# Feed-forward stage 1 with one 512-column matmul for the high weight part, and PSUM as four tiles of two banks

## The chip, the cores and the metric

The kernel runs on one core of one Trainium2 chip. The time is device microseconds of one execution. Before the change the median of three runs is 1102.05 us (1101.83 to 1103.43).

## The reference

Two layers of a decoder trunk, batch 1, 256 tokens (S), model width 1024 (D), all in float32. Layer 0 is a feed-forward block, native sparse attention (NSA) and a feed-forward block; layer 1 is a feed-forward block, differential attention and a feed-forward block:

```
x = x + 1/2 FFN1(rmsnorm(x)); x = x + Mixer(rmsnorm(x)); x = x + 1/2 FFN2(rmsnorm(x))

def swiglu(x, w_in, w_out):
    a, b = jnp.split(x @ w_in, 2, axis=-1)
    return (jax.nn.silu(a) * b) @ w_out
```

`w_in` is 1024 x 5632 (a gate half and an up half, 2816 each), `w_out` is 2816 x 1024. The change is in `x @ w_in`, which occurs four times, and in how PSUM is declared for the whole program.

## The kernel before

**Precision.** Every float32 product is made of three matmuls. A value is split in a high part (rounded to float32r) and a low part (value minus high part), and `mm3` issues high x high, low x high and high x low into the same accumulator (L359, L360, L361; `mm3x` is the same for stage 2 at L364 to L366).

**Weights.** `Stream` loads chunks of 128 x 2048 words by the SP queue into three buffers. ACT casts the high part (`whi`, L86, four pieces of 128x512), DVE and POOL make the low part (`wlo`, L89 and L91); how many columns of a piece go to POOL is set by `W.pool`, which is 0 in the inner pairs of a feed-forward block.

**Activations.** x is held transposed, as eight k-tiles of 128 rows by 256 tokens. `Norm` holds g * x as `xhi` and `xlo`, two tiles. 1/rms is applied after stage 1, by multiplying with `rb`, which has the same row in every partition. `Norm.bank` makes the parts of two k-tiles (ACT `xhi` L327, DVE `xlo` L328), the squares (ACT L334) and their sum (POOL L336, L338).

**Feed-forward (`ffn`).** The 2816 hidden units are 11 pairs p of 256. `stage1(p)` is 8 k-tiles x 2 halves j of the pair x gate and up (c) x three matmuls of 256 columns: 96 matmuls into two PSUM banks, each with gate and up side by side. The banks alternate: 4 and 5 for even p, 6 and 7 for odd p. `evac(p)` multiplies a bank by `rb` on DVE (`ab`, L401), takes Silu on ACT (`sh`, L403), multiplies by the up half on DVE (L405), and splits the result in `hh` (ACT, L407) and `hl` (DVE, L409). `stage2(p)` is 48 matmuls of 256 columns that add to banks 0 to 3 over all pairs (24 of 512 columns in the last block). The program issues stage1(p), evac(p), stage2(p-1) for each p, so on TensorE the stage 2 of one pair lies between two stages 1, and evac(p) has that time to come through. At the end of a block `residual_bank` adds each bank to x (DVE, L370) and calls `Norm.bank` for the next stage.

**Order and PSUM.** The framework orders the instructions of each engine by the priorities that come from program order, and places the semaphore waits from the tiles that the instructions read and write. PSUM is eight tiles of one bank, `B[0]` to `B[7]`. The mixers use the same tiles. In NSA `kc_t` transposes the compressed keys into `B[2 + tb]`, bank 2 and bank 3 in turn (L618), and DVE adds a position term out of that bank (`kc`, L622); the head loops transpose probabilities (L882) into one bank while DVE and ACT copy from others (L884, L885, L904).

Of the kernel before, what the change touches and what calls it, by code (L numbers as in the profile page):

```python
# [17 lines left out]
P = 128  # L18
# [38 lines left out]
class Stream:  # L57
    """Weight chunks of 128 x 2048 words, loaded and split ahead of their use."""

# [64 lines left out]
def trunk_kernel(ctx, tc, x, ffn1_norm, ffn1_w_in, ffn1_w_out, mix_norm, ffn2_norm, ffn2_w_in, ffn2_w_out,  # L124
# [10 lines left out]
    pp = pool("pp", 1, space=bass.MemoryType.PSUM)  # L135
    B = [pp.tile([P, 512], F32, name=f"bank{i}") for i in range(8)]

# [159 lines left out]
    def rsqrt(h, n, out=None, np_=P):  # L297
        """1 / sqrt(-2 h), for h < 0."""
        y, a = out if out is not None else tiny("ry", n)[:np_], (tiny if n <= 32 else t2)("ra", n)[:np_]
        nc.vector.tensor_scalar(y.bitcast(I32), h.bitcast(I32), -0.5, 0x5F1FFFF9 - 0x40400000, op0=ALU.mult, op1=ALU.add)  # L300
        beta = 3 * 0.703952253
        nc.vector.scalar_tensor_tensor(a, y, beta, y, op0=ALU.mult, op1=ALU.mult)
        nc.vector.tensor_tensor(a, a, h, op=ALU.mult)
        nc.vector.scalar_tensor_tensor(y, a, beta * 2.38924456 / 2, y, op0=ALU.add, op1=ALU.mult)
        nc.vector.scalar_tensor_tensor(a, y, 4.0 / 9.0, y, op0=ALU.mult, op1=ALU.mult)
        nc.vector.tensor_tensor(a, a, h, op=ALU.mult)
        nc.vector.scalar_tensor_tensor(a, a, 5.0 / 3.0, a, op0=ALU.add, op1=ALU.mult)
        nc.vector.scalar_tensor_tensor(y, a, 1.25, y, op0=ALU.add, op1=ALU.mult)
        return y

    class Norm:
        """Holds g * x^T as two float32r parts, and 1 / rms of each token."""

        def __init__(self, g0):
            self.g0 = g0
            self.hi = xp.tile([P, KT, S], F32R, tag="xhi", name=nm("xhi"))
            self.lo = xp.tile([P, KT, S], F32R, tag="xlo", name=nm("xlo"))
            self.acc = t2("acc")
# [21 lines left out]
        def rms(self, ps):  # L340
            """1 / rms as a column."""
            for tb in range(2):
# [7 lines left out]
        def rms_row(self, ps):  # L350
            """1 / rms along the free dimension, the same in every partition."""
            nc.tensor.matmul(ps[:, :S], ones, self.acc[:, :S], start=True, stop=True)
# [20 lines left out]
    def ffn(nrm, nxt_g, last=False, first=False):  # L373
        hbuf = {}
        xn = None

        def stage1(p):
            gs = [B[4 + 2 * (p % 2)], B[5 + 2 * (p % 2)]]
            for half in range(2):
# [3 lines left out]
                for kk in range(4):  # L383
                    k = half * 4 + kk
                    for j in range(2):
                        for c in range(2):
                            mm3(gs[j][:, c * S:(c + 1) * S], hv[:, kk, c, j * P:(j + 1) * P], lv[:, kk, c, j * P:(j + 1) * P],
                                nrm.hi[:, k, :], nrm.lo[:, k, :], k == 0 and c == 0, k == KT - 1)
                    if p == 0 and k == (7 if first else 6):
                        nrm.rms_row(B[0])  # L390
                    if p == 1 and k == (3 if first else 1):
                        evac(0)

        def evac(p):
            gs = [B[4 + 2 * (p % 2)], B[5 + 2 * (p % 2)]]
            hh = halves(t2("hh", 512, F32R), 2)
# [3 lines left out]
            for j in range(2):  # L400
                nc.vector.tensor_tensor(halves(ab[j], 2), halves(gs[j], 2), nrm.rb[:, None, :].to_broadcast([P, 2, S]), op=ALU.mult)  # L401
            for j in range(2):
# [9 lines left out]
        def stage2(p, nxt=None):  # L412
# [5 lines left out]
            if last:  # L418
                for tb, c0, c1 in ((0, 0, 512), (0, 512, 1024), (1, 0, 512)) + (((1, 512, 768), (1, 768, 1024)) if end else ((1, 512, 1024),)):
                        yb = B[2 * tb + c0 // 512][:, c0 % 512:c0 % 512 + c1 - c0]  # L420
# [9 lines left out]
                return  # L430
            for d in range(KT):
                for j in range(2):
                    mm3x(B[d // 2][:, (d % 2) * S:(d % 2 + 1) * S], hv[:, j, d * P:(d + 1) * P], lv[:, j, d * P:(d + 1) * P],
                        hh[:, j, :], hl[:, j, :], p == 0 and j == 0 and d % 2 == 0, end and j == 1)
                if end and d % 2:
                    residual_bank(d // 2, 0.5, nxt)

        for p in range(NPAIR):
            W.pool = FFN_SPLIT if p in (0, NPAIR - 1) or first and p == 1 else 0
            stage1(p)  # L440
            if p:
                evac(p)
            if p == NPAIR - 1 and first:
                setup_late2(B[4 + 2 * ((p + 1) % 2)])
            if p == 0 and last:
# [9 lines left out]
            if p:  # L455
                stage2(p - 1)
        if last:
            stage2(NPAIR - 1)
# [5 lines left out]
    def proj(key, nrm, segs, split):  # L464
        """Yields after each tile of the model dimension; segs[tb]: (psum, width, opens its bank)."""
        tot = sum(sg[1] for sg in segs[0])
# [34 lines left out]
    def qk_factors(b, nrm, r2, fac):  # L501
        """Per token and head of the raw projection: the norm's factor, and its inverse."""
        ss = tiny("ss", 16)
# [96 lines left out]
    def nsa(nrm, nxt_g):  # L600
# [209 lines left out]
        def filler():  # L810
            for k in proj("q1", nrm, full(0), (4, 4)):
                yield
            qhl1 = q_parts(0, xp.tile([P, 2048], F32R, tag="xlo", name=nm("qhl")), 1)
            yield
# [343 lines left out]
```

## Time and profile before

| | us |
|---|---|
| median of 3 runs | 1102.05 |
| span of the profiled execution | 1109.3 |
| TensorE (PE) busy | 1066.8 (96%) |
| DVE busy | 786.5 (71%) |
| ACT busy | 563.8 (51%) |
| POOL busy | 297.9 (27%) |
| mean granted TensorE clock | 0.973 of full speed |

The profiled execution has no time of its own beside its span: the span, from its first to its last instruction, is 1109.3 us, 7.25 us (0.7%) above the median of the runs. PE's busy time includes overlap of neighbouring matmuls, so the distance from one matmul's start to the next says more than a matmul's duration.

### The profile page before, as it was taken

The page shows a single profiled execution, that of the slowest core. Times are in us where ns is not written, and L with a number is a line of the kernel's source. Part 1 is how long each engine was busy: PE and PEld are TensorE (multiplying, and loading weights), DVE is VectorE, ACT ScalarE, POOL GpSimd, SP SyncE. Part 2 cuts the span into 40 slices and gives each one's busy share as a digit, 9 for nine tenths or more (in the row PEclk, how much of TensorE's full clock was granted, in tenths as well). Part 3 has the DMA queues.
Part 4 walks back from the last instruction along what each step waited for, and adds up shares of the span by engine and source line. Part 5 has one row for each costly group of instructions (what it writes and reads, how often), then busy time and mean ns, then how long its engine had stood idle before and what let it go on. Part 6 is the DMA issues. An engine that isn't in the chain of part 4 may idle for free.

```text
span 1109.3 us, 20061 instructions
## 1 busy us (share of the span) xinstructions
PE 1066.8 (96%) x7766; PEld 992.1 (89%) x7766; DVE 786.5 (71%) x1638; ACT 563.8 (51%) x1231; POOL 297.9 (27%) x350
## 2 busy tenths in 40 slices
PE   8899999998899999999999999999998989999998
PEld 7799999877767899999999999998776689999997
DVE  6865655889887796655689556568877789565664
ACT  6344444546587654444455444446454456444442
POOL 5500001766653240000073000017575434000002
PEclk9899999998899999999999999999998799999999
DMA  7655564477411256565565655654533225656551
GB/s 231 201 191 191 183 198 159 145 152 203 146 39 39 77 170 211 184 196 182 163 188 170 210 191 161 198 174 157 190 115 113 77 77 166 203 165 198 182 189 39
DMA packets 129980, 178.20 MB, mean 161 GB/s; under 512 B 5162, under 2 KB 104668, under 8 KB 129884
## 3 DMA queue, kind: packets, MB, share of 16 engines
q1 hardware_dynamic: 129708, 176.84, 50.4%
q8 instruction: 61, 1.00, 0.4%
q14 instruction: 35, 0.29, 0.1%
q10 hardware_dynamic: 176, 0.07, 0.0%
HBM read 175.84 MB, written 1.05 MB: 159 GB/s over the span
## 4 chain that ended last, share of the span: by engine, by line
PE 75%; DVE 17%; issue 3%; ACT 3%; POOL 1%; DMA 1%; SPq 0%; ACTq 0%; POOLq 0%; DVEq 0%
PE bank L360 18%; PE bank L359 18%; PE bank L361 18%; DVE wlo L89 6%; PE bank L366 5%; PE bank L364 5%; PE bank L365 5%; PE bank L901 1%; DVE xlo L328 1%; ACT whi L86 1%; PE bank L882 1%; PE bank L1038 1%; PE bank L849 1%; DMA xnat<-in_x_dram 1%; DVE kc L622 1%
## 5 line engine op out<-in xcount | busy, mean ns | idle before, releaser
L89 DVE TENSOR_TENSOR wlo<-raw,whi 128x512 fp32r<-128x512 f32 (+5 forms) x661 | 429.8, 688 | 189.0 <-ACT whi L86 187.7
L86 ACT CAST whi<-raw 128x512 fp32r<-128x512 f32 (+1 forms) x661 | 374.8, 618 | 362.8 <-issue 325.0
L91 POOL TENSOR_TENSOR wlo<-raw,whi 128x320 fp32r<-128x320 f32 (+4 forms) x240 | 229.9, 983 | 718.0 <-ACT whi L86 713.4
L361 PE MATMUL bank<-xhi,wlo 128*128 128x256 f32 x1408 | 397.7, 283 | 0.0
L360 PE MATMUL bank<-xlo,whi 128*128 128x256 f32 x1408 | 397.7, 282 | 0.0
L359 PE MATMUL bank<-xhi,whi 128*128 128x256 f32 x1408 | 397.7, 283 | 0.0
L359 PEld LDWEIGHTS bank<-xhi,whi 128*128 128x128 f32 x1408 | 266.1, 189 | 0.7 <-ACT xhi L327 0.2
L360 PEld LDWEIGHTS bank<-xlo,whi 128*128 128x128 f32 x1408 | 265.7, 189 | 0.7 <-DVE xlo L328 0.2
L361 PEld LDWEIGHTS bank<-xhi,wlo 128*128 128x128 f32 x1408 | 265.7, 189 | 0.0
L364 PE MATMUL bank<-hh,whi 128*128 128x256 f32 x528 | 150.5, 285 | 4.1 <-ACT hh L407 4.1
L366 PE MATMUL bank<-hl,whi 128*128 128x256 f32 x528 | 150.6, 285 | 1.3 <-DVE hl L409 1.3
L365 PE MATMUL bank<-hh,wlo 128*128 128x256 f32 x528 | 150.0, 284 | 0.0
L401 DVE TENSOR_TENSOR ab<-bank,rb 128x512 f32<-128x512 f32 x88 | 60.3, 691 | 67.6 <-PE bank L361 66.7
L364 PEld LDWEIGHTS bank<-hh,whi 128*128 128x128 f32 x528 | 102.0, 193 | 4.4 <-ACT hh L407 4.3
L366 PEld LDWEIGHTS bank<-hl,whi 128*128 128x128 f32 x528 | 101.9, 193 | 1.9 <-DVE hl L409 1.9
L365 PEld LDWEIGHTS bank<-hh,wlo 128*128 128x128 f32 x528 | 102.0, 193 | 0.0
L359 PE MATMUL bank<-whi,xhi 128*128 128x512 f32 (+1 forms) x192 | 78.9, 411 | 1.2 <-DVE kTl L645 1.2
L360 PE MATMUL bank<-wlo,xhi 128*128 128x512 f32 (+1 forms) x192 | 76.3, 398 | 3.0 <-DVE wlo L89 3.0
L361 PE MATMUL bank<-whi,xlo 128*128 128x512 f32 (+1 forms) x192 | 76.0, 396 | 0.0
L529 ACT ACTIVATE p<-p,mn 128x128 f32<-128x128 f32 (+1 forms) x96 | 43.0, 450 | 26.0 <-DVE mn L528 25.7
L403 ACT ACTIVATE sh<-ab 128x256 f32<-128x256 f32 x88 | 36.4, 413 | 23.0 <-DVE ab L401 23.0
L360 PEld LDWEIGHTS bank<-wlo,xhi 128*128 128x128 f32 x192 | 38.4, 200 | 10.3 <-issue 3.9
(242 smaller groups left out, 1274.7 us busy)
## 6 DMA issues: line engine op xcount, KB each, us to landing
raw<-in_ffn_w_in_dram SPq DMA_DIRECT2D x174, 512.0 KB, 4.8
raw<-in_ffn_w_out_dram SPq DMA_DIRECT2D x44, 1024.0 KB, 4.9
raw<-in_diff_w_in_dram SPq DMA_DIRECT2D x12, 1024.0 KB, 5.3
raw<-in_nsa_w_in_dram SPq DMA_DIRECT2D x6, 1024.0 KB, 5.2
raw<-in_nsa_cmp_w_dram SPq DMA_DIRECT2D x8, 512.0 KB, 7.1
raw<-in_nsa_w_out_dram SPq DMA_DIRECT2D x4, 1024.0 KB, 5.4
raw<-in_diff_w_out_dram SPq DMA_DIRECT2D x4, 1024.0 KB, 5.0
raw<-in_nsa_w_in_dram SPq DMA_DIRECT2D x4, 512.0 KB
```

The source lines that it names most:

```text
L86: self.nc.scalar.copy(hi[:, a:b], raw[:, a:b])
L89: self.nc.vector.tensor_tensor(lo[:, a:m], raw[:, a:m], hi[:, a:m].bitcast(F32), op=ALU.subtract)
L91: self.nc.gpsimd.tensor_tensor(lo[:, m:b], raw[:, m:b], hi[:, m:b].bitcast(F32), op=ALU.subtract)
L359: nc.tensor.matmul(ps, wh, xh, start=start, stop=False, skip_group_check=True)
L360: nc.tensor.matmul(ps, wh, xl, start=False, stop=False, skip_group_check=True)
L361: nc.tensor.matmul(ps, wl, xh, start=False, stop=stop, skip_group_check=True)
L364: nc.tensor.matmul(ps, wh, xh, start=start, stop=False, skip_group_check=True)
L365: nc.tensor.matmul(ps, wl, xh, start=False, stop=False, skip_group_check=True)
L366: nc.tensor.matmul(ps, wh, xl, start=False, stop=stop, skip_group_check=True)
L401: nc.vector.tensor_tensor(halves(ab[j], 2), halves(gs[j], 2), nrm.rb[:, None, :].to_broadcast([P, 2, S]), op=ALU.mult)
L403: nc.scalar.activation(sh[j][:, :S], ab[j][:, :S], AF.Silu)
L529: nc.scalar.activation(p, p, AF.Exp, bias=mn, scale=-1.0, accum_out=sm)
```

## The change

PSUM is declared as four tiles of two banks (`pair`), and `B[i]` is now a half of such a tile. The high and low parts of g * x become one tile `both`, in which the two parts of a k-tile lie side by side, 512 columns.

For p of 1 and up, stage 1 issues two matmuls instead of three for each k-tile, j and c: the high weight part times high and low activations together, 512 columns into a whole bank, and the low weight part times the high activations, 256 columns into the first half of that bank. A pair then takes four banks: one pair tile per j, gate in its first bank and up in its second. Those tiles are banks 4 to 7 for every p from 2 on (banks 0, 1, 6, 7 for p = 1), where before two sets alternated. In `evac` ACT first copies the low halves of a pair tile into `sh`, DVE adds them to the other halves, and the multiplication by `rb` then reads the sum from SBUF. Pair 0 keeps the three matmuls, into banks 4 and 5.

Around it: `rms_row` uses bank 2; stage2(0) begins with banks 2 and 3; the last stage 2 of a block runs all eight d for j = 0 first and then for j = 1 with the residuals; `setup_late2` (the transposes at L271 and L273) moves behind stage2(9); in `nsa` a buffer takes the new tag and size.

```diff
-    B = [pp.tile([P, 512], F32, name=f"bank{i}") for i in range(8)]
+    pair = [pp.tile([P, 1024], F32, name=f"bank{2 * i}") for i in range(4)]
+    B = [pair[i // 2][:, i % 2 * 512:(i % 2 + 1) * 512] for i in range(8)]
...
-            self.hi = xp.tile([P, KT, S], F32R, tag="xhi", name=nm("xhi"))
-            self.lo = xp.tile([P, KT, S], F32R, tag="xlo", name=nm("xlo"))
+            self.both = xp.tile([P, KT, 2, S], F32R, tag="xhl", name=nm("xhl"))
+            self.hi, self.lo = self.both[:, :, 0], self.both[:, :, 1]
...
+        def gate_up(p):
+
+            return [pair[0] if p == 1 else pair[2], pair[3]]
+
...
-                            mm3(gs[j][:, c * S:(c + 1) * S], hv[:, kk, c, j * P:(j + 1) * P], lv[:, kk, c, j * P:(j + 1) * P],
-                                nrm.hi[:, k, :], nrm.lo[:, k, :], k == 0 and c == 0, k == KT - 1)
+                            wh, wl = hv[:, kk, c, j * P:(j + 1) * P], lv[:, kk, c, j * P:(j + 1) * P]
+                            if p == 0:
+                                mm3(B[4 + j][:, c * S:(c + 1) * S], wh, wl,
+                                    nrm.hi[:, k, :], nrm.lo[:, k, :], k == 0 and c == 0, k == KT - 1)
+                                continue
+                            g = gate_up(p)[j][:, c * 512:(c + 1) * 512]
+                            nc.tensor.matmul(g, wh, nrm.both[:, k].rearrange("p c t -> p (c t)"),
+                                             start=k == 0, stop=False, skip_group_check=True)
+                            nc.tensor.matmul(g[:, :S], wl, nrm.hi[:, k, :], start=False, stop=k == KT - 1,
+                                             skip_group_check=True)
                     if p == 0 and k == (7 if first else 6):
-                        nrm.rms_row(B[0])
+                        nrm.rms_row(B[2])
...
-                nc.vector.tensor_tensor(halves(ab[j], 2), halves(gs[j], 2), nrm.rb[:, None, :].to_broadcast([P, 2, S]), op=ALU.mult)
+                src = halves(B[4 + j], 2)
+                if p:
+                    g = gate_up(p)[j].rearrange("p (c x t) -> p c x t", c=2, x=2)
+                    nc.scalar.copy(halves(sh[j], 2), g[:, :, 1])
+                    nc.vector.tensor_tensor(halves(ab[j], 2), g[:, :, 0], halves(sh[j], 2), op=ALU.add)
+                    src = halves(ab[j], 2)
+                nc.vector.tensor_tensor(halves(ab[j], 2), src, nrm.rb[:, None, :].to_broadcast([P, 2, S]), op=ALU.mult)
...
+            order = [*range(4, KT), *range(4)] if p == 0 else [*range(KT)]
+            for js in ((0,), (1,)) if end else ((0, 1),):
+                for d in order:
+                    for j in js:
+                        mm3x(B[d // 2][:, (d % 2) * S:(d % 2 + 1) * S], hv[:, j, d * P:(d + 1) * P], lv[:, j, d * P:(d + 1) * P],
+                             hh[:, j, :], hl[:, j, :], p == 0 and j == 0 and d % 2 == 0, end and j == 1)
+                    if end and j == 1 and d % 2:
+                        residual_bank(d // 2, 0.5, nxt)
```

**The evacuation of a pair on DVE.** Inside the first block, between two stages 1, DVE works on one pair's banks and on pieces of the next chunks (`wlo15` is one of those). Before:

```order
L401 TENSOR_TENSOR ab_40_1113<-bank4_86,rb_12_340 128x512
L401 TENSOR_TENSOR ab_41_1114<-bank5_87,rb_12_340 128x512
L89 TENSOR_TENSOR wlo15_1128<-raw15_939,whi15_1127 128x512
L405 TENSOR_TENSOR sh_42_1115<-sh_42_1115,ab_40_1113 128x256
L89 TENSOR_TENSOR wlo15_1128<-raw15_939,whi15_1127 128x512
L405 TENSOR_TENSOR sh_43_1116<-sh_43_1116,ab_41_1114 128x256
L409 TENSOR_TENSOR hl_39_1112<-sh_42_1115,hh_38_1111 128x256
L89 TENSOR_TENSOR wlo15_1128<-raw15_939,whi15_1127 128x512
L409 TENSOR_TENSOR hl_39_1112<-sh_43_1116,hh_38_1111 128x256
```

With the change, at the same pair (L416 is the added sum, L418 the multiplication by `rb`, L422 and L426 are the old L405 and L409):

```order
L416 TENSOR_TENSOR ab_39_992<-bank4_84,sh_41_994 128x512
L89 TENSOR_TENSOR wlo15_1011<-raw15_850,whi15_1010 128x512
L418 TENSOR_TENSOR ab_39_992<-ab_39_992,rb_11_335 128x512
L416 TENSOR_TENSOR ab_40_993<-bank6_85,sh_42_995 128x512
L422 TENSOR_TENSOR sh_41_994<-sh_41_994,ab_39_992 128x256
L418 TENSOR_TENSOR ab_40_993<-ab_40_993,rb_11_335 128x512
L426 TENSOR_TENSOR hl_38_991<-sh_41_994,hh_37_990 128x256
L89 TENSOR_TENSOR wlo15_1011<-raw15_850,whi15_1010 128x512
L422 TENSOR_TENSOR sh_42_995<-sh_42_995,ab_40_993 128x256
L89 TENSOR_TENSOR wlo15_1011<-raw15_850,whi15_1010 128x512
L426 TENSOR_TENSOR hl_38_991<-sh_42_995,hh_37_990 128x256
```

Two sums have come in, the last reads of the banks are now the two sums, and `hl` stands two operations further back.

**The end of a block on DVE.** After the last stage 2 of the first block DVE adds the banks to `xT` (L370) and makes the low parts (L328), with pieces of the next weights between. Before:

```order
L370 SCALAR_TENSOR_TENSOR xT_104<-bank0_82,xT_104 128x512
L89 TENSOR_TENSOR wlo34_2397<-raw34_2190,whi34_2396 128x192 x2
L328 SCALAR_TENSOR_TENSOR xlo_81_2394<-xT_104,gcol_94,xhi_80_2393 128x256
L370 SCALAR_TENSOR_TENSOR xT_104<-bank1_83,xT_104 128x512
L328 SCALAR_TENSOR_TENSOR xlo_81_2394<-xT_104,gcol_94,xhi_80_2393 128x256
L370 SCALAR_TENSOR_TENSOR xT_104<-bank2_84,xT_104 128x512
L328 SCALAR_TENSOR_TENSOR xlo_81_2394<-xT_104,gcol_94,xhi_80_2393 128x256 x4
L370 SCALAR_TENSOR_TENSOR xT_104<-bank3_85,xT_104 128x512
```

With the change (L371 and L329 are the old L370 and L328; `bank0` and `bank2` are tiles of two banks):

```order
L89 TENSOR_TENSOR wlo34_2111<-raw34_1933,whi34_2110 128x192 x3
L371 SCALAR_TENSOR_TENSOR xT_100<-bank0_82,xT_100 128x512
L371 SCALAR_TENSOR_TENSOR xT_100<-bank2_83,xT_100 128x512
L329 SCALAR_TENSOR_TENSOR xhl_79_2108<-xT_100,gcol_90,xhl_79_2108 128x256 x2
L371 SCALAR_TENSOR_TENSOR xT_100<-bank0_82,xT_100 128x512
L329 SCALAR_TENSOR_TENSOR xhl_79_2108<-xT_100,gcol_90,xhl_79_2108 128x256 x2
L371 SCALAR_TENSOR_TENSOR xT_100<-bank2_83,xT_100 128x512
```

The weight pieces now stand ahead of the first residual, and the second residual is that of the other pair tile: TensorE finishes bank 0, then bank 2, then banks 1 and 3.

**The transposes of the compressed keys on TensorE.** In the NSA prelude four sets of four transposes (L618) lie between the matmuls of the key projection (`whi36` is its second chunk). The first two sets before the change:

```order
L618 MATMUL bank2_84<-cst_91,kcn_90_2590 128x128 x4
L359 MATMUL bank6_88<-whi36_2532,xhi_80_2393 128x512
L360 MATMUL bank6_88<-wlo36_2533,xhi_80_2393 128x512
L361 MATMUL bank6_88<-whi36_2532,xlo_81_2394 128x512
L359 MATMUL bank7_89<-whi36_2532,xhi_80_2393 128x512
L360 MATMUL bank7_89<-wlo36_2533,xhi_80_2393 128x512
L361 MATMUL bank7_89<-whi36_2532,xlo_81_2394 128x512
L618 MATMUL bank3_85<-cst_91,kcn_90_2590 128x128 x4
```

With the change (L638 is the old L618), the second and the third set:

```order
L638 MATMUL bank2_83<-cst_87,kcn_88_2304 128x128 x4
L360 MATMUL bank6_85<-whi36_2246,xhl_79_2108 128x512
L361 MATMUL bank6_85<-wlo36_2247,xhl_79_2108 128x512
L362 MATMUL bank6_85<-whi36_2246,xhl_79_2108 128x512
L360 MATMUL bank6_85<-whi36_2246,xhl_79_2108 128x512
L361 MATMUL bank6_85<-wlo36_2247,xhl_79_2108 128x512
L362 MATMUL bank6_85<-whi36_2246,xhl_79_2108 128x512
L360 MATMUL bank6_85<-whi36_2246,xhl_79_2108 128x512
L638 MATMUL bank2_83<-cst_87,kcn_88_2304 128x128 x4
L361 MATMUL bank6_85<-wlo36_2247,xhl_79_2108 128x512
L362 MATMUL bank6_85<-whi36_2246,xhl_79_2108 128x512
```

Between the first and the second set nine matmuls stand now instead of six, and between the later ones seven. All four sets write the one tile `bank2`, in its first or its second bank, and in the built program each set from the second on carries a wait for DVE's reads of the set before it; before, the third and the fourth set waited for the reads of the set two before, in the same bank. The same kind of wait, for reads of the other bank of a pair tile, stands at 53 matmuls or transposes of TensorE, 21 instructions of ACT and 6 of DVE in the changed program; with eight tiles there was none.

## Rows read from the trace of the kernel before

**Rows 1.** The page: engines, and the chain that ended last.

```profile
PE 1066.8 (96%) x7766; PEld 992.1 (89%) x7766; DVE 786.5 (71%) x1638; ACT 563.8 (51%) x1231; POOL 297.9 (27%) x350
PE 75%; DVE 17%; issue 3%; ACT 3%; POOL 1%; DMA 1%; SPq 0%; ACTq 0%; POOLq 0%; DVEq 0%
```

**Rows 2.** Windows: PE, PEld, DVE, ACT, POOL busy us, clock, DMA share, GB/s.

```profile
60.00:120.00 60.00, 60.00 (x507) 60.00 (x506) 36.47 (x66) 28.08 (x59) 0.00 (x0) 1.00 0.58 183
560.00:620.00 60.00, 60.00 (x502) 59.80 (x501) 51.90 (x84) 33.23 (x69) 24.35 (x24) 1.00 0.61 193
220.00:300.00 80.00, 69.08 (x379) 59.18 (x380) 72.98 (x152) 43.63 (x84) 53.43 (x68) 0.89 0.62 163
300.00:400.00 100.00, 96.58 (x661) 77.63 (x660) 80.17 (x293) 70.93 (x216) 43.25 (x63) 1.00 0.20 63
840.00:900.00 60.00, 50.31 (x236) 38.98 (x237) 41.98 (x138) 28.09 (x69) 26.54 (x35) 0.80 0.23 71
```

**Rows 3.** Timeline of PE: stage 1 (90 us), stage 2 of the last block, projection.

```profile
89.74 0.28 PE L361 MATMUL bank<-xhi,wlo 128*128 128x256 f32 x1
...
91.17 0.28 PE L361 MATMUL bank<-xhi,wlo 128*128 128x256 f32 x1
...
1060.30 0.39 PE L359 MATMUL bank<-whi,hh 128*128 128x512 f32 x1
...
1065.79 0.28 PE L359 MATMUL bank<-xhi,whi 128*128 128x256 f32 x1
...
228.78 0.39 PE L361 MATMUL bank<-whi,xlo 128*128 128x512 f32 x1
...
230.86 0.39 PE L361 MATMUL bank<-whi,xlo 128*128 128x512 f32 x1
```

**Rows 4.** Groups by line and shape: busy us, mean ns, idle time before and its releaser.

```profile
L401 DVE TENSOR_TENSOR ab<-bank,rb 128x512 f32<-128x512 f32 x88 | 60.3, 691 | 67.6 <-PE bank L361 66.7
L328 DVE SCALAR_TENSOR_TENSOR xlo<-xT,gcol,xhi 128x256 fp32r<-128x256 f32 x40 | 31.0, 805 | 1.3 <-ACT xhi L327 0.8
L370 DVE SCALAR_TENSOR_TENSOR xT<-bank,xT 128x512 f32<-128x512 f32 x20 | 13.5, 680 | 2.8 <-PE bank L361 2.8
L885 DVE COPY pT<-bank 128x256 f32<-128x256 f32 x16 | 6.7, 422 | 6.1 <-PE bank L882 6.0
L884 ACT COPY pT<-bank 128x512 f32<-128x512 f32 x16 | 9.3, 578 | 3.7 <-PE bank L882 3.6
```

**Rows 5.** Timeline of DVE, then of PE, at the end of the first block.

```profile
197.84 1.40 DVE L401 TENSOR_TENSOR ab<-bank,rb 128x512 f32<-128x512 f32 x2 [0.98 <-PE bank L361]
...
203.32 0.41 DVE L409 TENSOR_TENSOR hl<-sh,hh 128x256 fp32r<-128x256 f32 x1
...
206.98 0.68 DVE L370 SCALAR_TENSOR_TENSOR xT<-bank,xT 128x512 f32<-128x512 f32 x1
...
215.16 0.68 DVE L370 SCALAR_TENSOR_TENSOR xT<-bank,xT 128x512 f32<-128x512 f32 x1
...
220.79 0.61 PE L343 MATMUL bank<-ones,acc 128*128 128x2 f32 x4 [1.65 <-POOL acc L338]
```

**Rows 6.** Timeline of PE, then of DVE, at the key transposes.

```profile
232.94 0.60 PE L618 MATMUL bank<-cst,kcn 128*128 128x128 f32 x4
...
237.32 0.70 PE L618 MATMUL bank<-cst,kcn 128*128 128x128 f32 x4 [2.37 <-DVE kc L622]
...
234.51 1.03 DVE L622 TENSOR_TENSOR kc<-bank,gcol 64x512 f32<-64x512 f32 x1
...
236.35 4.15 DVE L622 TENSOR_TENSOR kc<-bank,gcol 64x448 f32<-64x448 f32 x4
```

**Rows 7.** Timeline of DVE, then of PE, at the end of the last block.

```profile
1093.78 1.41 DVE L401 TENSOR_TENSOR ab<-bank,rb 128x512 f32<-128x512 f32 x2 [1.25 <-PE bank L361]
...
1096.08 0.98 DVE L409 TENSOR_TENSOR hl<-sh,hh 128x256 fp32r<-128x256 f32 x2
...
1105.26 0.39 PE L359 MATMUL bank<-whi,hh 128*128 128x256 f32 x1 [0.52 <-DVE yo L427]
```

More of the change, by code (lines that the diff above doesn't have):

```diff
@@ L375, in ffn @@
         xn = None
+        def gate_up(p):
+            return [pair[0] if p == 1 else pair[2], pair[3]]
         def stage1(p):
-            gs = [B[4 + 2 * (p % 2)], B[5 + 2 * (p % 2)]]
             for half in range(2):
@@ L394, in evac @@
         def evac(p):
-            gs = [B[4 + 2 * (p % 2)], B[5 + 2 * (p % 2)]]
             hh = halves(t2("hh", 512, F32R), 2)
@@ L418, in stage2 @@
             if last:
-                for tb, c0, c1 in ((0, 0, 512), (0, 512, 1024), (1, 0, 512)) + (((1, 512, 768), (1, 768, 1024)) if end else ((1, 512, 1024),)):
+                todo = ((0, 0, 512), (0, 512, 1024), (1, 0, 512)) + (((1, 512, 768), (1, 768, 1024)) if end else ((1, 512, 1024),))
+                for tb, c0, c1 in todo[2:] + todo[:2] if p == 0 else todo:
                         yb = B[2 * tb + c0 // 512][:, c0 % 512:c0 % 512 + c1 - c0]
@@ L430, in stage2 @@
                 return
[L431 to L436, printed above, removed]
+            order = [*range(4, KT), *range(4)] if p == 0 else [*range(KT)]
[6 more added lines that the diff above has]
+                        residual_bank(d // 2, 0.5, nxt)
         for p in range(NPAIR):
@@ L442, in ffn @@
                 evac(p)
-            if p == NPAIR - 1 and first:
-                setup_late2(B[4 + 2 * ((p + 1) % 2)])
             if p == 0 and last:
@@ L456, in ffn @@
                 stage2(p - 1)
+            if p == NPAIR - 1 and first:
+                setup_late2(B[4])
         if last:
@@ L812, in filler @@
                 yield
-            qhl1 = q_parts(0, xp.tile([P, 2048], F32R, tag="xlo", name=nm("qhl")), 1)
+            qhl1 = q_parts(0, xp.tile([P, 4096], F32R, tag="xhl", name=nm("qhl"))[:, :2048], 1)
             yield
```

## Prediction

> **What bounds the kernel now.** I read the page first, then windows by stage, then the timeline of TensorE for its pace, then that of DVE at the seams. The page shows PE busy 96% of the span and on 75% of the chain that ended last, DVE on 17% [rows 1]. The windows say where each holds. In the inner pairs of a feed-forward block PE has no gap: 60.00 of 60 us busy, 507 matmuls, while DVE works 36.5 and ACT 28.1 us of the 60, POOL nothing, at clock 1.00 [rows 2]. There the number and width of the matmuls alone set the time. In the two mixers PE has gaps (69.1 of 80 us in the NSA prelude, 96.6 of 100 in the NSA heads, 50.3 of 60 in differential attention), and its clock is lower on average in two of the three (0.89 and 0.80) [rows 2]; there a wait for DVE or ACT can lie on the path. So the change meets two kinds of stage: in the first it takes matmuls away, in the second it only changes which PSUM tile a wait is for.
>
> **What is removed.** Per k-tile, j and c, two matmuls of 256 columns become one of 512: 4 blocks x 10 pairs x 32 = 1280 such groups. The columns stay the same, so the gain is only what a matmul costs beyond its columns. The pace is the distance between starts: in stage 1 twelve steps in 1.43 us (119 ns) [rows 3], or 60 us / 507 = 118.3 ns in the window [rows 2]. Two cost 236.6 ns. For 512 columns two stretches bound the price: the 24 matmuls of a stage 2 in the last block, 5.49 us or 228.8 ns each, and the projection with nine steps in 2.08 us, 231.1 ns [rows 3]. A group thus saves 7.8 or 5.5 ns, the program 10.0 or 7.0 us; with 119 ns on the left side instead of 118.3 the first becomes 11.9. I take **-10.0 us**, from the stretch that lies, like the new stage 1, inside a feed-forward block with POOL idle; the bounds are -7.0 and -11.9.
>
> The Trainium skill, on its page TensorE: Matmul & The Clock Gate, section "Wait — 56ns, not 53.3ns?", gives a warm matmul its columns at 2.4 GHz and a fixed cost of about 2.5 ns. By that, an estimate, a group would save 2.5 ns and the program 3.2 us instead of 10.0. The trace does not agree with the page's figure: its 118.3 ns for 256 columns and 228.8 for 512 leave 11 and 15 ns beyond the columns, and the difference of the two, not either one, decides.
>
> **What is added in a pair.** ACT makes two copies of 128x512 out of PSUM (578 ns for such a copy, L884), DVE two sums of 128x512 that read PSUM (691 ns, L401) [rows 4]. That is 1.2 us of ACT and 1.4 us of DVE per pair of some 17 us; over 60 us some 3.5 pairs, DVE goes from 36.5 to about 41.4 and ACT from 28.1 to 32.2. I cost both at nothing in the inner pairs. The cover is stage 2 of the pair before, 48 x 118.3 ns = 5.7 us. Two things hang on it, since each pair from 2 on uses the same banks 4 to 7. First, the next stage 1 may overwrite the banks only after the sums have read them: copy 0.58, sum 0.69, one weight piece and one multiplication of some 0.7 each between, second sum 0.69, together 3.4 us after the last matmul, 2.3 us before the banks are needed. Second, `hh` and `hl` are needed only by the stage 2 after the next stage 1, over 10 us later. If that cover were gone, each 0.1 us short would cost 4 us over 40 pairs.
>
> **The seams of the blocks.** In the last pair there is no further stage 1 behind which `hl` can hide. Now `hl` of the second half is done at 203.73, 5.9 us after the first bank read at 197.84 [rows 5]. The added copy and sums (0.58 + 2 x 0.69 = 2.0 us) make it 7.9; the first half is 0.65 us earlier. Stage 2 wants the first half about 0.4 + 5.7 + 0.2 = 6.3 us after that bank read, so it may wait 0.9 us there, and in the first block alone some 1 us more, because the moved transposes stand among its first matmuls and wait for a DVE copy queued behind `hl`. The order by j puts the first residual behind 30 of the 48 matmuls instead of 12: 18 x 0.118 = 2.1 us later. Against that, DVE needed 8.2 us from the first to the last residual (206.98 to 215.16 [rows 5]), with weight pieces between; in the new order these stand ahead of it, and three residuals (0.68) and four low parts (0.81) [rows 4] make 5.3, which gives back 2.9. TensorE waited 1.65 us for the squares at the end of this [rows 5], and what hangs on the last residual comes 0.9 + 1.0 + 2.1 - 2.9 = 1.1 us later in the first block. Without the moved transposes it is 0.1 in the seam before differential attention. The seam between the two layers has no gap now (60.00 of 60 us busy [rows 2]); there PE needs the first two banks' low parts at once and those of bank 1 some 5 us after the second half's first bank is done, where my count of DVE's queue gives 5.4 to 6.9: a wait of 0.4 to 1.9 behind the 0.9. The bounds for the three are 0.3 and 6 us; I take **+2.2**: 1.1, 0.1 and 1.0.
>
> **Waits for the other bank of a pair tile.** 53 instructions of PE now wait for a read of a bank that they don't touch. The trace of before has no such wait, so I bound it. Below: nothing, where other work or another wait covers it. Above: the read that is waited for, 0.42 to 0.69 us (L885, L401) [rows 4], times those that stand in mixers and at seams.
> - Key transposes: now the second set goes ahead (232.94), and the third waits 2.37 us for two `kc` operations that stand behind weight pieces on DVE and end at 237.3 [rows 6]. With one tile the second set waits there, after nine matmuls of the projection instead of twelve: 3 x 0.231 = 0.7 us more idle. The third then waits for two more of about 1 us and the fourth again, each with seven matmuls (1.6 us) to cover 2 us. I take **+1.5**, 0.7 to 3.
> - NSA key, query and head part: 27 waits or so. At 0.42 us each that would be 11, at nothing 0. PE is 96.6% busy there, with matmuls of the next projection issued between [rows 2], so nearest to hidden: **+1.5**, bounds 0 and 5.
> - Differential attention, 13 waits, PE 84% busy [rows 2]: most add to idle time that is already there: **+1.5**, bounds 0 and 5.
> - Start: the transposes of x, two waits for a low part: **+0.3**, up to 1.5.
> - Last block: `hl` ended 3.3 us after the first bank read (1093.78 to 1097.06); with 2.0 more it is 5.3, against 6.0 to the last stage 2 (0.5 to the end of stage 1 and 24 x 0.229), so hidden. PE waited 0.52 us for an output's read (1105.26) [rows 7]; two of its waits are now for the other bank: **+0.5**, up to 1.5.
>
> **Sum.** -10.0 + 2.2 + 1.5 + 1.5 + 1.5 + 0.3 + 0.5 = -2.5 us against the profiled 1109.3. The median of the runs is 7.25 us lower; I take the same difference there: 1102.05 - 2.5 = **1099.5 us**. A change under 0.2% (2.2 us) would not be told from none in this measurement, so the forecast lies just outside.
>
> **The rivals.**
> - The waits stay covered. For it: PE has work from the next projection between most of them, and a read of 0.4 us can be over before PE arrives. Against it: the key transposes show that DVE's queue can hold a read back for over 3 us [rows 6]. With costs of 1 to 3 us and 10 to 11.9 gained: about 1093.5.
> - The waits cost more than the matmuls give: slower. The place is the two head loops, where DVE's and ACT's reads chain with PE's transposes; from 12.2 us of costs in all it decides. At 4 us each in NSA and differential attention and 2.5 at the key transposes the costs are 13.5 and, with 7.0 gained (the projection's pace), 1108.5; with 10.0 gained 1105.5.
> - The wide matmul saves little. No row shows a 512-column matmul with a 256-column one behind it in turn; if half of the projection's saving is lost in that alternation, 1280 x 2.75 ns = 3.5 us are gained, and with 7.5 of costs it is 1106. For it: the projection's 231 ns is already close to twice 118. Against it: 24 matmuls from 1060.30 to 1065.79 [rows 3]. The page of the Trainium skill named above would put the gain at about this size.
>
> **How the numbers follow.** Forecast, with its own range 1097 to 1102: 0.42. Waits covered: 0.25. Waits dearer: 0.22. Small gain: 0.11. The forecast's 0.42 lies half on either side of the 0.2%: 0.21 faster, 0.21 same. The covered case is faster whole; the two others are slower but for 0.01 each. Faster 0.21 + 0.25 = 0.46, same 0.23, slower 0.31. The range goes from 1092 (11.9 gained, 2 lost) to 1109 (7.0 gained, 13.9 lost).
>
> **What would show it.** Stage 1 of an inner pair should fall from 96 x 118.3 = 11.36 us to 32 x (228.8 + 118.3) = 11.11, PE staying gapless; if it is 11.3 the gain is the small one, and if gaps stand before a stage 1, the banks were not free and the cover failed. At the key transposes PE should wait before the second set, about 3 us. In the head loops the sum of idle time before transposes and score matmuls tells the first two rivals apart. If the seams of blocks show more than 3 us in one place, my count of DVE's queue is wrong; if the total moves by more than 10 us either way, something outside these terms (the clock in the stages with gaps) did it.

## The result, and the profile after

The changed kernel takes 1136.74 us (median of 4 runs, 1135.09 to 1138.24) against 1101.94 (4 runs, 1101.37 to 1103.43): 1.0294 times as long, interval 1.0257 to 1.0331. Forecast were 1099.5 in a range of 1092 to 1109.

The page after, PE and the engines' shares first, then the chain that ended last:

```profile
PE 1070.5 (94%) x6486; PEld 930.4 (82%) x6486; DVE 829.3 (73%) x1718; ACT 614.8 (54%) x1311; POOL 300.3 (27%) x350
PE 75%; DVE 18%; ACT 3%; issue 2%; DMA 1%; POOL 0%; SPq 0%; ACTq 0%; DVEq 0%
```

Beside [rows 1], 1280 matmuls are gone and PE is busy as long as before; nothing on the page says where 35 us went. It has to be read by stage. Between blocks and mixers stand the matmuls that sum the squares (L343 and L352 before, L344 and L353 after), so the distance from one to the next is a stage. Worked out from their starts, in us, with the last two columns from the sum of squares before NSA to the last `kc` sum, and from there to NSA's first residual ("heads": the key, query and value part and then the loop over the heads):

```
              start   FFN1     NSA    FFN2  FFN1(1)    diff    last  | to last kc   heads
before        23.69 197.10  176.94  189.21   189.52  149.56  183.31  |  22.50       138.9
after         27.75 194.34  198.40  190.52   187.49  151.93  182.88  |  26.28       158.3
difference    +4.06  -2.76  +21.46   +1.31    -2.03   +2.37   -0.43  |  +3.78       +19.4
```

The traces differ by 24.0 us, the times by 34.8. After the change every execution's time is 1.7 to 1.8 us above its span (1135.09 and 1133.3). The profiled span of before, 1109.3, was above its runs; in the later comparisons the runs of before go from 1099.55 to 1110.97, so it lies at their upper end. Where it differs shows beside experiment e3, which has the same work and a span of 1100.6: 7.1 of the 8.7 us are in differential attention (142.42 against 149.56), at a mean clock of 0.94 there against 0.90. Differences of a few us in that stage are therefore not explained here. But the seven traces with eight tiles in this document have 142.4 to 149.6 us there, the changed kernel 151.9: beside e3 it loses 9.5 us in that stage too, and most of the 10.8 us that the times differ by beyond the traces may stand there.

Windows after, columns as in [rows 2]; the second is the NSA heads:

```profile
60.00:120.00 60.00, 60.00 (x404) 55.39 (x404) 40.41 (x73) 32.50 (x65) 0.00 (x0) 1.00 0.58 189
...
305.00:407.00 102.00, 89.17 (x524) 63.58 (x524) 66.56 (x277) 59.41 (x193) 30.68 (x49) 0.92 0.16 52
```

The inner pairs are still gapless (60.00 of 60); the heads are not, and their mean clock has fallen to 0.92. The timeline of PE there, with e3's at the same place behind it:

```profile
375.02 0.41 PE L362 MATMUL bank<-oh,wlo 128*128 128x256 f32 x1
...
377.65 0.28 PE L866 MATMUL bank<-kTl,qT 128*128 128x256 f32 x1
379.57 0.70 PE L914 MATMUL bank<-pcT,vb 128*128 128x256 f32 x2 [1.64 <-DVE mn L548]
380.11 0.29 PE L902 MATMUL bank<-cst,p 128*128 128x128 f32 x1
380.33 1.12 PE L921 MATMUL bank<-pT,vn 128*64 128x256 f32 x2
381.38 0.48 PE L902 MATMUL bank<-cst,p 128*128 128x128 f32 x1
381.78 1.12 PE L921 MATMUL bank<-pT,vn 128*64 128x256 f32 x2
...
388.74 0.80 PE L360 MATMUL bank<-oh,whi 128*128 128x256 f32 x2 [0.46 <-ACT oh L923]
```

```profile
361.48 1.51 PE L901 MATMUL bank<-pT,vn 128*64 128x256 f32 x14
362.92 0.39 PE L360 MATMUL bank<-ol,whi 128*128 128x256 f32 x1
363.14 0.28 PE L361 MATMUL bank<-oh,wlo 128*128 128x256 f32 x1
363.26 0.28 PE L359 MATMUL bank<-oh,whi 128*128 128x256 f32 x1
...
367.29 0.65 PE L901 MATMUL bank<-pT,vn 128*64 128x256 f32 x2
```

In e3 14 matmuls on the values follow each other in 1.51 us, and output-projection matmuls (`oh`, `ol`) come behind them. After the change PE waits 1.64 us, starts no output-projection matmul from 375.02 to 388.74, and does the matmuls on the values in twos, between transposes of the next head. Two of them take 1.12 us there; in e3, where two stand alone, they take 0.65 us (367.29). So both the changed order and the clock lengthen this stretch. The granted clock was 0.50 from 373.4 to 376.8 us, 1.00 to 380.2 and 0.50 again to 390.5 (the two levels are 2.4 and 1.2 GHz): ahead of the first fall the engine had waited 0.46 and 1.35 us, ahead of the second 0.52 and 1.64. What PE waited for in the heads after the change (us in total, times, longest), the two largest for transposes:

```profile
PE bank L902 <- ACT p L893: 2.5, 1, 2.5
PE bank L902 <- DVE pT L905: 2.4, 2, 2.2
```

At the key transposes, PE, then DVE, to be held against [rows 6]:

```profile
239.56 0.63 PE L638 MATMUL bank<-cst,kcn 128*128 128x128 f32 x4 [4.47 <-DVE kc L642]
...
236.68 1.02 DVE L642 TENSOR_TENSOR kc<-bank,gcol 64x512 f32<-64x512 f32 x1
...
238.51 0.91 DVE L642 TENSOR_TENSOR kc<-bank,gcol 64x448 f32<-64x448 f32 x1
```

### The profile page after: what moved, and what is told of

It is laid out like the page before. It is cut to its first block, busy times and chain, and to the rows that moved or that the text cites. A ratio compares the mean times of both kernels' runs of the same rounds, so it can differ in the third digit from the quotient of the medians.

```text
span 1133.3 us, 17778 instructions
## 1 busy us (share of the span) xinstructions
PE 1070.5 (94%) x6486; PEld 930.4 (82%) x6486; DVE 829.3 (73%) x1718; ACT 614.8 (54%) x1311; POOL 300.3 (27%) x350
## 4 chain that ended last, share of the span: by engine, by line
PE 75%; DVE 18%; ACT 3%; issue 2%; DMA 1%; POOL 0%; SPq 0%; ACTq 0%; DVEq 0%
PE bank L397 25%; PE bank L399 13%; DVE wlo L89 6%; PE bank L360 5%; PE bank L361 5%; PE bank L362 5%; PE bank L367 5%; PE bank L365 5%; PE bank L366 5%; PE bank L921 1%; ACT whi L86 1%; DVE p L548 1%; PE bank L902 1%; DVE xhl L329 1%; DVE ab L418 1%
## 5 line engine op out<-in xcount | busy, mean ns | idle before, releaser
L397 PE MATMUL bank<-xhl,whi 128*128 128x512 f32 x1280 | 452.4, 394 | 0.0
L399 PE MATMUL bank<-xhl,wlo 128*128 128x256 f32 x1280 | 362.5, 283 | 0.0
L397 PEld LDWEIGHTS bank<-xhl,whi 128*128 128x128 f32 x1280 | 241.2, 188 | 54.1
L399 PEld LDWEIGHTS bank<-xhl,wlo 128*128 128x128 f32 x1280 | 241.5, 189 | 0.4
L416 DVE TENSOR_TENSOR ab<-bank,sh 128x512 f32<-128x512 f32 x80 | 54.9, 687 | 90.7 <-ACT sh L415 90.7
L415 ACT COPY sh<-bank 128x512 f32<-128x512 f32 x80 | 46.7, 584 | 106.8 <-PE bank L399 106.7
L360 PE MATMUL bank<-whi,xhl 128*128 128x512 f32 (+2 forms) x192 | 78.1, 407 | 3.1 <-DVE kTl L665 2.0
L361 PE MATMUL bank<-wlo,xhl 128*128 128x512 f32 (+2 forms) x192 | 76.6, 399 | 1.2 <-DVE wlo L89 1.2
L362 PE MATMUL bank<-whi,xhl 128*128 128x512 f32 (+2 forms) x192 | 75.8, 396 | 0.0
L418 DVE TENSOR_TENSOR ab<-ab,rb 128x512 f32<-128x512 f32 x80 | 59.4, 743 | 0.0
L420 ACT ACTIVATE sh<-ab 128x256 f32<-128x256 f32 x88 | 36.6, 417 | 32.5 <-DVE ab L418 32.5
L424 ACT CAST hh<-sh 128x256 fp32r<-128x256 f32 x88 | 35.5, 406 | 31.3 <-DVE sh L422 31.3
```

The costliest lines, as they stand in the source:

```text
L360: nc.tensor.matmul(ps, wh, xh, start=start, stop=False, skip_group_check=True)
L361: nc.tensor.matmul(ps, wh, xl, start=False, stop=False, skip_group_check=True)
L362: nc.tensor.matmul(ps, wl, xh, start=False, stop=stop, skip_group_check=True)
L397: nc.tensor.matmul(g, wh, nrm.both[:, k].rearrange("p c t -> p (c t)"), start=k == 0, stop=False, skip_group_check=True)
L399: nc.tensor.matmul(g[:, :S], wl, nrm.hi[:, k, :], start=False, stop=k == KT - 1, skip_group_check=True)
L418: nc.vector.tensor_tensor(halves(ab[j], 2), src, nrm.rb[:, None, :].to_broadcast([P, 2, S]), op=ALU.mult)
```

## The experiments

**Which part of the change.** e1 is the kernel before with the PSUM declaration alone, e2 the changed kernel without it, e3 and e4 two other parts alone.

```diff
e1 (in before)
-    B = [pp.tile([P, 512], F32, name=f"bank{i}") for i in range(8)]
+    pair = [pp.tile([P, 1024], F32, name=f"bank{2 * i}") for i in range(4)]
+    B = [pair[i // 2][:, i % 2 * 512:(i % 2 + 1) * 512] for i in range(8)]
e2 (in after, with the eight tiles of before)
-                    nc.scalar.copy(halves(sh[j], 2), g[:, :, 1])
-                    nc.vector.tensor_tensor(halves(ab[j], 2), g[:, :, 0], halves(sh[j], 2), op=ALU.add)
+                    for c in range(2):
+                        g, cs = gate_up(p)[j][c], slice(c * S, (c + 1) * S)
+                        nc.scalar.copy(sh[j][:, cs], g[:, S:])
+                        nc.vector.tensor_tensor(ab[j][:, cs], g[:, :S], sh[j][:, cs], op=ALU.add)
e3 (in before)
-            self.hi = xp.tile([P, KT, S], F32R, tag="xhi", name=nm("xhi"))
-            self.lo = xp.tile([P, KT, S], F32R, tag="xlo", name=nm("xlo"))
+            self.both = xp.tile([P, KT, 2, S], F32R, tag="xhl", name=nm("xhl"))
+            self.hi, self.lo = self.both[:, :, 0], self.both[:, :, 1]
e4 (in before: the new stage2 order, rms_row and setup_late2)
-                        nrm.rms_row(B[0])
+                        nrm.rms_row(B[2])
...
+            order = [*range(4, KT), *range(4)] if p == 0 else [*range(KT)]
+            for js in ((0,), (1,)) if end else ((0, 1),):
```

> The kernel before with nothing changed but PSUM declared as four tiles of two banks. If the waits for the other bank of a pair tile are the cause, this alone loses 25 to 35 us (1127 to 1137), most of it in the NSA heads; if the cause is elsewhere (one tile for high and low parts, the order at the block ends, the single set of banks), it stays within 3 us of 1102.

> The changed kernel with eight tiles of one bank, so that no wait is for another bank; gate and up of a pair are then copied and summed bank by bank (two copies and two sums of 128x256 instead of one of 128x512). If the pair tiles are the cause, the loss in the mixers goes and the wide matmul's 5.4 ns per group (350.7 ns measured against 356.1) remain: 6.9 us minus 1 to 3 us at the block ends, 1096 to 1099. If the cause is elsewhere it stays above 1120.

> The kernel before with only the high and low parts of the activations in one tile (and the NSA buffer that shares its place). That place has one buffer, so the next owner waits for the last reads of both parts. If the pair tiles are the cause: within 2 us of 1102. If the shared place is the cause: 5 to 30 us more, at the seams of blocks and in the NSA heads.

> The kernel before with only the order of the block ends changed (last stage 2 by halves, first stage 2 from banks 2 and 3, the late transposes behind the stage 2 before the last, the row sum in bank 2). If the pair tiles are the cause: within 2 us of 1102 (my prediction's sum for the seams without the added sums is 0 to +1). If the order is: 5 us or more lost, at the seams.

Measured, against 1103.1 of before on the same chip: e1 1138.31 (ratio 1.0331, 1.0296 to 1.0366; just above its range), e2 1098.67 (0.9963, 0.9942 to 0.9985), e3 1102.33 (0.9997, 0.9979 to 1.0014), e4 1104.44 (1.0015, 0.9995 to 1.0035). The declaration alone loses what the whole change loses and a little more; without it the change gains 0.4%. The shared tile and the order at the block ends are no cause of the loss. Windows of the NSA heads, e3 first, then e1:

```profile
300.00:381.00 81.00, 78.94 (x520) 60.54 (x521) 63.74 (x271) 59.61 (x193) 30.60 (x49) 1.00 0.20 65
```

```profile
306.00:409.00 103.00, 90.32 (x525) 65.13 (x524) 66.53 (x277) 59.21 (x193) 30.62 (x49) 0.90 0.16 52
```

Nearly the same matmuls (525 and 520) take 103 us instead of 81. PE is idle for 12.7 instead of 2.1 us, 10.6 more; and it is busy for 11.4 us more, at a mean clock of 0.90 instead of 1.00. At two levels, half and full, 0.90 means a fifth of the 103 us at half speed, which costs about 10 us. So the slower clock cost about as much again as the idle time. That the idle time brought the clock down is argued from the order of events; no run changes one without the other.

**What the wide matmul gives, and the block ends.** f4 is e2 with the wide matmul cut in two, f3 is e2 with the last stage 2 of a block in the old order.

```diff
f4 (in e2)
-                            nc.tensor.matmul(g, wh, nrm.both[:, k].rearrange("p c t -> p (c t)"),
-                                             start=k == 0, stop=False, skip_group_check=True)
+                            nc.tensor.matmul(g[:, :S], wh, nrm.hi[:, k, :], start=k == 0, stop=False,
+                                             skip_group_check=True)
+                            nc.tensor.matmul(g[:, S:], wh, nrm.lo[:, k, :], start=False, stop=k == KT - 1,
+                                             skip_group_check=True)
f3 (in e2)
-            for js in ((0,), (1,)) if end else ((0, 1),):
+            for js in ((0, 1),):
...
-                    if end and j == 1 and d % 2:
+                    if end and d % 2:
```

> The changed kernel with eight tiles (as e2), but the 512-column matmul of stage 1 replaced by two of 256 columns into the two halves of the same bank; copies, sums and order stay. The difference to e2 is what the wide matmul alone gives: 6.9 us by the 5.4 ns per group that the trace after the change shows (1105 to 1106 here), 10 us by the term of my prediction (1108 to 1109), 3.2 us by the fixed cost of the Trainium skill's page on TensorE (1102).

> The changed kernel with eight tiles (as e2), and the last stage 2 of a block in the old order, both halves of each d together. If the split by halves hides the later hl, as my step on the seams has it, this loses 1 to 4 us against e2 (1100 to 1103); if the split only makes the first residual later, it gains 1 to 4 (1095 to 1098).

Measured against 1103.23: f4 1106.54 (1.0027, 1.0003 to 1.0051), f3 1095.6 (0.9933, 0.9904 to 0.9963). From e2 to f4 the ratio moves by 0.0064, about 7 us, but with both intervals it may be 3.5 to 10.6, which hardly tells the three sizes apart; the four feed-forward stages of the two traces differ by 8.6 us (749.87 and 758.48 in sum). The pace in the trace after the change, eight groups of a wide and a narrow matmul from 88.86 to 91.66:

```profile
88.86 0.39 PE L397 MATMUL bank<-xhl,whi 128*128 128x512 f32 x1
89.08 0.28 PE L399 MATMUL bank<-xhl,wlo 128*128 128x256 f32 x1
89.20 0.40 PE L397 MATMUL bank<-xhl,whi 128*128 128x512 f32 x1
...
91.66 0.40 PE L397 MATMUL bank<-xhl,whi 128*128 128x512 f32 x1
```

A group takes 350 ns there; three matmuls took 357 at the 119 ns of [rows 3] and 355 at the window's 118.3. That is 5 to 7 ns each, 6.4 to 9 us for 1280, in agreement with f4. f3 came out in the range of its second case, a gain. It is the fastest of all kernels here; whether it is really ahead of e2 the intervals leave open. Their traces stand within 0.1 us of each other before differential attention (769.6 and 769.5 us after the start): the split by halves brings the sum of squares forward in the feed-forward blocks, and NSA gives it back, most of it at the key transposes, where PE waits 4.5 us in e2 for `kc` sums that stand behind weight pieces on DVE, and 2.4 in f3.

**Which pair, and whether waits add up.** Kernels before, with only some banks as pair tiles (f1: banks 0 to 3, f2: 4 to 7, h0, h2, h4, h6: one pair, named by its first bank).

```diff
h2 (in before; the others accordingly)
-    B = [pp.tile([P, 512], F32, name=f"bank{i}") for i in range(8)]
+    pair = pp.tile([P, 1024], F32, name="bank2")
+    B = [pair[:, (i - 2) * 512:(i - 1) * 512] if i in (2, 3) else pp.tile([P, 512], F32, name=f"bank{i}") for i in range(8)]
```

> The kernel before with only banks 0 to 3 declared as two pair tiles, 4 to 7 as single ones. It keeps 40 of the 53 waits of TensorE for another bank. If the loss goes with the number of those waits, 25 to 30 of the 36 us are lost (1128 to 1133). If it sits in the later NSA heads, whose transposes go to banks 4 to 7, it is under 15 (below 1118).

> The kernel before with only banks 4 to 7 declared as two pair tiles. It keeps 13 of the 53 waits. By their number 6 to 11 us are lost (1109 to 1114); if the later heads are the place, over 20 (above 1123). If the two parts add up, f1 and this lose 36 us together; if an order of instructions that the two make together is the cause, less.

> The kernel before with only banks 0 and 1 declared as one pair tile (14 of the 53 waits of TensorE). These banks serve the start, the projections' and block ends' sums and the query transposes, not the heads' scores and probabilities. If only waits inside a head's chain (transposes, scores, values) matter: 1 to 5 us lost, at the start and in the prelude, NSA heads unchanged at 81 us. If any changed dependence that reorders the program costs: 8 us or more.

> The kernel before with only banks 2 and 3 as a pair tile (26 of the 53): key transposes and the transposes of the first five heads, whose first four blocks lie in bank 2 and whose last two in bank 3. Chain theory: 10 to 16 us lost, 2 to 3 at the key transposes, the rest in the first heads. By number of waits (36 x 26/53): 18.

> The kernel before with only banks 4 and 5 as a pair tile (1 of the 53, and 6 waits of ACT): scores of all heads in bank 4, of the even heads in bank 5. By number of TensorE's waits nothing is lost (1103). Chain theory: a head's transposes and the next scores then hold each other up through reads by ACT and DVE, 4 to 10 us in the later heads.

> The kernel before with only banks 6 and 7 as a pair tile (12 of the 53): scores and late transposes of the odd heads in bank 6, every head pair's output in bank 7. By number 8 us; chain theory 8 to 14, in the later heads, since a head's scores then wait until the output of the pair before has been read. If the four single pairs add up to more than the 36 of all four, their waits lie behind one another.

Measured, with two stages worked out as above. The last column counts the output-projection matmuls in each trace from the first transpose of a pair of heads (twelve transposes) to the first of the next pair, from the third pair on; the changed kernel has the counts of e1.

```
            us      ratio (interval)          to last kc  heads   output projection
e3       1102.33  0.9997 (0.9979..1.0014)       22.54     136.6   33 24 20 29 31 55
e1       1138.31  1.0331 (1.0296..1.0366)       25.27     159.7    8 51 37  6 30 60
f1       1131.64  1.0238 (1.0195..1.0280)       26.73     148.4   22 29 24 23 31 63
f2       1118.84  1.0141 (1.0099..1.0184)       21.84     157.2   22 45 29 12 30 54
h0       1119.20  1.0122 (1.0066..1.0177)       24.14     146.6   24 30 24 23 31 60
h2       1118.78  1.0130 (1.0086..1.0174)       26.27     136.2   33 21 20 29 31 58
h4       1114.72  1.0104 (1.0059..1.0149)       22.54     144.1   36 31 33  8 32 52
h6       1116.40  1.0109 (1.0070..1.0149)       21.83     147.9   28 31 34 15 29 55
```

The number of TensorE's waits does not set the loss: h4 has one of the 53 (and six waits of ACT) and loses 1%, h2 has 26, among them the transposes of the first five heads, and loses 1.3%, none of it in the heads (136.2). Its loss stands at the key transposes (+3.7 against e3) and above all in differential attention (157.8 us, beside 142.4 to 149.6 with eight tiles). f1 came out in the range that the number gave, f2 in neither of its ranges. Nor do the losses add up: by the ratios they are 26 us for f1 and 16 for f2, together 42, and 51 for the four single pairs, where all four pairs at once lose 36.

By what the expectations call the chain theory, only waits within a head's own chain of transposes, scores and values cost time. To hold that against the table, "heads" has to be split at the first transpose of probabilities, where the loop begins. The loop takes 76.4 us in e3, 97.5 in e1, 96.6 in the changed kernel, 83.5 in h4, 84.5 in h6, 76.3 in h2 and 78.9 in h0. So h4 and h6 lose 7 and 8 us there, as the theory had it, but h2 loses nothing where it had most of 10 to 16. Of the 10 us that h0 loses in "heads", 7.6 stand ahead of the loop, in the key, query and value part, and 2.5 in it, though banks 0 and 1 hold no scores or probabilities; in all it lost 13 us by the ratio, as its other case had it (8 or more from any dependence that reorders the program). In h4's loop PE is idle for 4.8 us instead of e3's 1.6 and the clock is 1.00 throughout, so a loss there does not need a slower clock. What goes with the loss is the last column: where the framework has kept nearly the order of the output projection (e3, h2) the heads take 136 us; where it has made another, 144 to 160. Whether the order causes the loss, the next two runs ask.

**Waits or order.** How many pieces of other work the program issues behind each head stands in a table of 16 numbers, written for the order that eight tiles give. k1 has the pair tiles and a table that brings the order nearly back, k2 eight tiles and a table that gives nearly the order of the pair tiles.

```diff
k1 (in e1)
-    NSA_FILL = [7, 1, 1, 3, 0, 2, 2, 0, 0, 1, 0, 3, 0, 3, 0, 5]
+    NSA_FILL = [7, 4, 0, 3, 0, 0, 2, 0, 1, 0, 1, 2, 1, 1, 1, 4]
k2 (in before)
+    NSA_FILL = [7, 1, 0, 2, 3, 1, 2, 0, 0, 0, 1, 2, 0, 2, 2, 6]
```

> The kernel with four pair tiles and nothing else (as e1), but with other numbers in the table that says how many pieces of other work stand behind each NSA head, so that the output-projection matmuls between the dozens of transposes are again near those of the kernel before: 30, 24, 26, 22, 32, 58 instead of 8, 51, 37, 6, 30, 60 (before: 33, 24, 20, 29, 31, 55). All waits stay in kind. If the order costs the heads their 22 us, most of it comes back: heads 136 to 146 us after the last key sum instead of 159.7, and 1118 to 1128 in all. If the waits themselves cost it, the heads stay above 154.

> The kernel before with its eight tiles and only that table changed, so that the output-projection matmuls between the dozens of transposes are near those with pair tiles: 13, 47, 35, 13, 32, 52 instead of 33, 24, 20, 29, 31, 55. No wait for another bank comes in. If the order costs: the heads lose 8 to 20 us (1111 to 1123). If the waits cost: under 4 us lost (below 1107).

Measured: k1 1135.02 (1.0274, 1.0244 to 1.0304), k2 1106.16 (1.0031, 1.0000 to 1.0061). In the heads: e3 136.6, k2 139.7, k1 150.6, e1 159.7. k2 came out as if the order cost little (under 4 us), k1 between its two cases (146 and 154). An order near that of the pair tiles costs 3 us where no wait is added; the waits with the order nearly restored cost 14; together they cost 23. The orders agree only by pairs of heads, though: from the fifth head on, head by head, k1 has 4 26 10 14 10 16 6 16 2 30 4 54 where e3 has 13 20 3 21 12 8 12 17 4 27 1 54, so a part of the 14 may still be order. (In k1's whole time only 3 us of the 9 come back; its trace has 151.85 us in differential attention against e1's 146.83.) What PE waited for in k1's heads, grouped (us in total, times, longest), the three largest:

```profile
PE bank L741 <- DVE qT L744: 2.6, 1, 2.6
PE bank L883 <- DVE mn L529: 2.0, 2, 1.4
PE bank L883 <- DVE ol L905: 1.7, 1, 1.7
```

The last of them is a transpose that waits until DVE has subtracted out of the bank next to its own: a wait by tile, 1.7 us where the read itself takes 0.42. What it waits for is mostly the queue in front of the read. In the loop k1 takes 88.4 us, e3 76.4: PE is idle for 10.4 instead of 1.6 us and busy for 78.0 instead of 74.8, so that 8.8 of the 12 us are idle time. The other 2 of the 14 stand ahead of the loop.

## Why the prediction was wrong

The forecast had the right mechanism among its costs and the wrong size for it, and one failed step decided: **"NSA key, query and head part ... +1.5, bounds 0 and 5"**. It measured 19.4 us between the two traces (column "heads"). The price was wrong three times over. First, each wait was bounded by the length of the read that it waits for, 0.42 to 0.69 us; what counts is when that read comes up in its engine's queue (single waits of 1.7 us in k1 and 2.2 after the change). Even at 0.42 us the prediction's 27 waits gave 11, and the bound was set at 5 because PE was 96.6% busy. Second, the matmuls of other work were taken as given cover, "with matmuls of the next projection issued between"; but the declaration changes the order in which the framework issues them, and in one place of the heads 29 output-projection matmuls became 6. By k2 another order alone costs 3 us. Third, idle time was priced at itself; with it came a clock at half, and PE was slower by about as much again (in e1, 10.6 us idle and 11.4 slower). The last sign in the prediction, a total off by more than 10 us, had named the clock in the stages with gaps. The rival "the waits cost more than the matmuls give" named the place and priced 4 us for it where 19 were lost, and had 0.22.

The other steps:
- Wide matmul, "-10.0" with bounds "-7.0 and -11.9": about 7 us by f4 (3.5 to 10.6), 6.4 to 9 by the pace. The lower bound, the projection's pace, was the right row. The figure of 2.5 ns on the Trainium skill's page TensorE: Matmul & The Clock Gate (section "Wait — 56ns, not 53.3ns?") would be 3.2 us, an estimate; the pace gives two to three times that.
- Copies and sums at nothing in the inner pairs: right. No gap in 60 us, with DVE at 40.4 and ACT at 32.5; predicted were 41.4 and 32.2.
- Seams, +2.2: not seen as a loss. In the first, DVE after the change, with PE behind it:

```profile
199.60 0.69 DVE L416 TENSOR_TENSOR ab<-bank,sh 128x512 f32<-128x512 f32 x1 [1.63 <-ACT sh L415]
...
206.25 0.41 DVE L426 TENSOR_TENSOR hl<-sh,hh 128x256 fp32r<-128x256 f32 x1
...
210.78 1.27 DVE L371 SCALAR_TENSOR_TENSOR xT<-bank,xT 128x512 f32<-128x512 f32 x2
...
214.23 0.68 DVE L371 SCALAR_TENSOR_TENSOR xT<-bank,xT 128x512 f32<-128x512 f32 x1
...
222.09 0.61 PE L344 MATMUL bank<-ones,acc 128*128 128x2 f32 x4 [0.49 <-POOL acc L339]
```

  From the first residual to the last it is 3.5 us instead of the 8.2 of [rows 5]; my count had 5.3. The stage as a whole is 2.8 us shorter, more than the wide matmul's quarter of 7; in e1, without the wide matmul, it is 1.4 us shorter, behind a later start. Only the seam between the layers got longer (+1.3 with that quarter gained); e1, which has none of the added sums, is 3.0 us longer there, so that this is more likely the pair tiles' than the late `hl`'s.
- Key transposes, "+1.5, 0.7 to 3", PE to wait before the second set "about 3 us": the place was right, the wait is 4.47 us, and the last `kc` sum comes 3.8 us later. Part of that is not the tiles': in e2 and e4, with eight tiles and the new block ends, it is 2 us later too, behind one wait each, of 4.5 and 4.6 us. e1 against before is +2.8.
- Start, "+0.3, up to 1.5": 4.06 us. e1 has 4.2 and e2 0.1, so it is the pair tiles. The transposes of x come in two sets of eight before (at 5.51 and 9.37 us) and in four sets of four after the change, the last at 15.04, and PE then waits 3.09 us for the sum of squares:

```profile
27.75 0.70 PE L353 MATMUL bank<-acc,ones 128*128 128x256 f32 x2 [3.09 <-POOL acc L339]
```

- Last block, +0.5: 0.43 shorter with 1.7 gained, a cost of 1.3. Differential attention, "+1.5, bounds 0 and 5": +2.4 between the two traces, but about 8 against the middle of the seven eight-tile kernels (142.4 to 149.6). Of the six kernels with pair tiles among banks 0 to 3, five have 151.85 to 157.8 us there and e1 146.8; the three with pair tiles among banks 4 to 7 alone lie within the eight tiles' range. So this term was probably too small as well. There is one trace of each kernel, and no run tests it.

## What to carry to other kernels

A tile is what the framework orders by, not a bank: declare as one tile only what is written and read together, and use a two-bank tile in one stage only if the others can keep their own. Where an order of work is tuned by a table of numbers, any new dependence in the program puts that table out of tune; count, before and after, the other work's matmuls per step of the loop. A changed count shows where the order has moved, though the new order alone cost only 3 us here. The number of added waits does not give the price: h4 with one of TensorE's lost 1%, h2 with 26 lost 1.3%. Price a wait by the queue in front of what it waits for, and reckon with a slower clock behind it, which in e1's heads cost as much again and in h4's loop nothing.

## What the runs showed of the hardware

A 512-column matmul followed by a 256-column one takes 350 ns here (88.86 to 91.66 us after the change), about 5 to 7 ns less than three of 256 columns; the weight loads that are saved (PEld busy 55.4 instead of 60.0 of 60 us) brought no more than that. TensorE's granted clock in the NSA heads was 1.00 with 2.1 us of idle time in 81 us (e3) and 0.90 with 12.7 us in 103 (e1). In the changed kernel it was at half from 373.4 to 376.8 us, behind waits of 0.46 and 1.35 us, and from 380.2 to 390.5, behind 0.52 and 1.64. In h4's loop over the heads it stayed at 1.00 with 4.8 us of idle time in 83.5.
